# Where the first column piece of v comes from: the normalised rows, or x times scale

## The chip, the cores and the metric

The kernel runs on one core of a Trainium2 chip. The core has a matrix engine (TensorE, here PE, whose weight loads are listed as PEld), a vector engine (DVE), a scalar engine for activations (ACT), a small general engine (POOL) and queues that start DMA transfers between the chip's main memory and the core's own memory (the SP queue carries most of them). Each engine runs its own instructions in the order in which the program was written out, and waits where an operand isn't there yet. The metric is the device time of one execution in microseconds.

## The reference

Two token groups, 1024 prompt rows and 32 sample rows of 1024 channels, go through a two-layer encoder. Only the first mixer's first half matters here:

```python
mod = jax.nn.silu(c) @ w_ada[i] + b_ada[i]
sh1, sc1, gt1, sh2, sc2, gt2 = jnp.split(mod[:, None, :], N_MOD, axis=-1)
h = rmsnorm(x, g_norm[i, 0]) * (1 + sc1) + sh1
z = jax.nn.gelu(h @ w_in)
u, v = jnp.split(z, 2, axis=-1)
v = rmsnorm(v, g_v)
```

`rmsnorm(x, g)` is x times the reciprocal root r of each row's mean square, times g. So a row of `h @ w` is r times (x times s) @ w, plus (shift @ w), where s = g * (1 + sc1) is one number a channel and the last term is the same row for every token of a group. Behind that come the gating of u by v, a pooling mixer in the second layer, and two squared-ReLU channel MLPs.

## The kernel before

**Arithmetic.** Each product of two matrices is made as three products in a reduced fp32 format: every operand is split into a high and a low half (`hh` and `hl` of the rows, `wh` and `wl` of the weights), and hh·wh, hl·wh and hh·wl are summed in PSUM. High halves are made on ACT, low halves on DVE as the difference.

**Tiles.** The 1056 rows stand channel by channel ("turned") in `acc` as three tiles: 384 rows, 384 rows, and 256 rows with the 32 sample rows. A tile has three row blocks, so there are nine, b = 0 to 8, of which block 8 is the sample. v has 2048 columns, in four pieces p of 512. One pair (p, b) is 24 products of 128 x 512 (8 channel blocks k, three products each), and 16 for block 8. The weights of a piece come as four quarters (p, q), of two channel blocks each.

**The order.** The start, up to the last part of the norm of tile 2, is written out by hand inside `tc.manual_schedule()` (from L991 on). Everything behind it is placed by a planner: it keeps a running estimate of PE's and DVE's time (`tick`, and the helpers of L66 to L84 through which nearly all DVE work goes, so that it is recorded under line 79), and puts work for later stages (`weave`: high and low halves of weights, slices of w_ada) between the products where DVE is thought to have time. Loads are issued in the order of one list, `stream`, as buffers come free (`issue`, L395).

**The start before, step by step.** The blocks of x are loaded in front (`add_x`), then for each quarter q the slice 4 + q of w_ada (scale), its slice q (shift) and a quarter of the weights. The conditions are passed through silu and turned (`turn_conditions`, csilT). A block of x is squared and summed on ACT (`x_squares`), and turned on PE in two halves of four transposes (`x_turn`, xT, L580), which DVE and ACT copy to `acc`. `first_norm(t)` makes the reciprocal root of each row (`spread`), puts these on the diagonal of a matrix (L730) and multiplies it with ones (pb_h, L732), which spreads them over all partitions; `apply` then makes, channel block by channel block, mt = x * scale * root on DVE, hh = mt + shift on ACT (L875) and hl on DVE. A slice of w_ada is 16 small products (ada, L477), a transposition on DVE (adas, L489) and eight small products (adat, L459), behind which coef (scale) or shift is made. `early_mm` (L973) makes the products of piece 0 for blocks 0 to 4 quarter by quarter as the norm proceeds; block 5 follows in one go (`v_mm`, L929 to L931), and `early_end` closes them (`v_end`: gelu, square and sum, store of vd by the SP queue, L941 to L943). The result tile `vt` of `v_end` has three buffers, and so has the small PSUM pool (`ps_ms`) that takes xT, ada, adat and pb_h. Behind the part by hand, `v_order` goes through piece 1 for blocks 0 to 5, pieces 0 and 1 for blocks 6 to 8, and then pieces 2 and 3.

Later slices of w_ada (from the ninth on) are made on DVE in place of PE: 16 multiplications by csil (aa), a transposition and a sum.

Of the kernel before, what the change touches and what calls it, by code (L numbers as in the profile page):

```python
# [15 lines left out]
P = 128  # L16
# [18 lines left out]
def tile_stream_encoder_step(  # L35
# [26 lines left out]
    act = nc.scalar.activation  # L62
# [10 lines left out]
    def on_dve(op, fixed, rate):  # L73
        def run(out, *args, **kw):
            n = 1
            for k in out.shape[1:]:
                n *= k
            time["dve"] += fixed + n / rate
            return op(out, *args, **kw)  # L79

        return run
# [98 lines left out]
    def load_vectors(i, part):  # L180
        at = sum(k for _, k in rows[i][: part.start])
        for ap, k in rows[i][part]:
            nc.scalar.dma_start(vec_rows[i][at : at + k, :P], ap)
            at += k
# [6 lines left out]
    def turn_conditions():  # L191
        raw = vec_rows[2]
        nc.vector.memset(csil32, 0.0)
        act(out=raw[0:16, P : 2 * P], in_=raw[0:16, :P], func=AF.Silu)

        act(out=raw[0:16, 2 * P : 2 * P + 1], in_=epsT[0:16, :], func=AF.Sqrt)
        pt = ps_ms("csilT")
        nc.tensor.transpose(pt[:, 0:16], raw[0:16, P : 2 * P], ident[0:16, 0:16])
# [3 lines left out]
    def turn_vectors():  # L202
        for raw, v in zip(vec_rows, vecs):
            n = v.shape[1]
            pt = ps_ms("rowT")
            nc.tensor.transpose(pt[:, :n], raw[:n, :P], ident[:n, :n])
            nc.vector.tensor_copy(v, pt[:, :n])
# [131 lines left out]
    for b in range(3):  # L339
        add_x(b)  # L340
    for q in range(4):
        for j in (8 + 2 * q, 9 + 2 * q, 2 * q, 2 * q + 1):
            add_ada(0, j)
        add_w(*v_item(0, q))
        if q == 0:
            for b in range(3, 6):
                add_x(b)
# [30 lines left out]
    state = {"issued": 0, "next": 0, "raw": 0, "used": 0, "folds": 0}  # L378
    deferred = []

    def in_raw(k):
# [5 lines left out]
    x_rows = [  # L387
        room("h", t, f"x_rows{t}")
        .rearrange("p k n -> p (k n)")[:, : ncol[t] // P * D]
        .rearrange("p (b k n) -> p b k n", k=KB, n=P)  # L390
        for t in range(NT)
    ]
    junk = room("l", NT - 1, "xsq")

    def issue():  # L395
        while state["issued"] < len(stream):
            k = state["issued"]
            kind, key, ap, shape = stream[k]
            if in_raw(k):
                if state["raw"] == RAW_SLOTS:  # L400
                    return
                state["raw"] += 1
                r = t_raw(f"raw{k}")
            elif kind == "x":
                r = x_rows[key // 3][:, key % 3] if key < 8 else junk[:, :, P : 2 * P]
            else:
                r = work.tile([P, 1024], F32, tag="W", bufs=W_SLOTS, name=f"raw{k}")
            if kind == "x":
                nr = P if key < 8 else DEC
                i = (nc.scalar if key == 2 else nc.sync).dma_start(  # L410
                    r[:nr], ap.rearrange("t (k n) -> t k n", n=P)
                )
            else:
                i = nc.sync.dma_start(r.rearrange("p (a b) -> p a b", a=shape[0]), ap)
            raws[k] = r
            loads[key] = i.ins
            state["issued"] += 1

    def do_w(key, r):
# [4 lines left out]
        if key == ("v", 0, 0):  # L424
            late_lo.append(lambda: tt(out=wl, in0=r, in1=wh.bitcast(F32), op=ALU.subtract))
        else:
            tt(out=wl, in0=r, in1=wh.bitcast(F32), op=ALU.subtract)
# [135 lines left out]
    def x_squares(b, r):  # L563
# [8 lines left out]
    def x_turn(b, r):  # L572
# [3 lines left out]
        for half in range(2):  # L576
# [8 lines left out]
            if half == 0 or t == 0:  # L585
# [5 lines left out]
    x_turns = deque()  # L591

    def do_x(b, r):
        x_squares(b, r)
        if b < 3:
            x_turn(b, r)
        else:
            x_turns.append(lambda: x_turn(b, r))
# [10 lines left out]
    def stream_step():  # L609
# [18 lines left out]
        if in_raw(k):  # L628
# [85 lines left out]

    def spread(t, ss, tag, out, dg):
# [5 lines left out]
        ts(ms[:, :nb], ss[:, :nb], 1.0 / D, EPS, op0=ALU.mult, op1=ALU.add)  # L721
        act(out=r0[:, :nb], in_=ms[:, :nb], func=AF.Sqrt)
        nc.vector.reciprocal(out=r0[:, :nb], in_=r0[:, :nb])
        tt(out=q[:, :nb], in0=r0[:, :nb], in1=r0[:, :nb], op=ALU.mult)
        stt(out=q[:, :nb], in0=q[:, :nb], scalar=-0.5, in1=ms[:, :nb], op0=ALU.mult, op1=ALU.mult)
        stt(out=r0[:, :nb], in0=q[:, :nb], scalar=1.5, in1=r0[:, :nb], op0=ALU.add, op1=ALU.mult)
        yield False
        pb = ps_ms(f"pb_{tag}")
        for b, (c0, w) in enumerate(blk):
            act(out=dg[:w, c0 : c0 + w], in_=ident[:w, :w], func=AF.Copy, scale=r0[:w, b : b + 1])  # L730
        for b, (c0, w) in enumerate(blk):
            mm(pb[:, c0 : c0 + w], ones[:w, :], dg[:w, c0 : c0 + w], start=True, stop=True)  # L732
        out.append(pb)
# [119 lines left out]
    def apply(t, l, cf, sh, r, keep=False):  # L853
        hh[t] = room("h", t, f"hh{l}_{cf}_{t}", F32R)
        hl[t] = room("l", t, f"hl{l}_{cf}_{t}", F32R)
# [40 lines left out]

    def products(ps, n, terms):
# [8 lines left out]

    ssqv = small.tile([P, 9, 4], F32, name="ssqv")
# [51 lines left out]
    h0, h1, h2 = (first_norm(t) for t in range(NT))  # L959

    def early_mm(bs, q):

        wh, wl = witem[("v", 0, q)]
        for second in (False, True):
            for b in bs:
                t, c0 = b // 3, b % 3 * P
                tick(0.46 if second else 0.92)
                for k in range(2):
                    kb = 2 * q + k
                    a_h, a_l = hh[t][:, kb, c0 : c0 + P], hl[t][:, kb, c0 : c0 + P]  # L970
                    w = slice(k * 512, k * 512 + 512)
                    for a in (a_h,) if second else (a_h, a_l):
                        mm(  # L973
                            early_ps[b],
                            a,
                            (wl if second else wh)[:, w],
                            start=kb == 0 and a is a_h and not second,
                            stop=kb == KB - 1 and second,
                        )
# [5 lines left out]
    def conditions(q):  # L985

        stream_to("ada", (0, 4 + q, 1))
        stream_to("ada", (0, q, 1))
        pe_folds.pop(0)()

    with tc.manual_schedule():  # L991
        load_vectors(2, slice(0, 2))
        issue()
        load_vectors(2, slice(2, 4))
        load_vectors(0, slice(0, 1))
        load_vectors(1, slice(0, 1))
        turn_conditions()
        stream_to("x", 1)
        turn_vectors()
        stream_to("x", 2)  # L1000
        next(h0)
        conditions(0)
        statistics(h0)
        stream_to("w", ("v", 0, 0))
        pe_folds.pop(0)()
        for q in range(4):
            next(h0)
            if q == 0:
                late_lo.pop()()
            early_mm((0, 1, 2), q)  # L1010
            if q == 0:
                stream_to("x", 5)
                next(h1)
                x_turns.popleft()()
                x_turns.popleft()()
                next(h1)
                x_turns.popleft()()
                statistics(h1)
            next(h1)
            if q < 3:  # L1020
                conditions(q + 1)
                stream_to("w", ("v", 0, q + 1))
                early_mm((3,), q)
                pe_folds.pop(0)()
                early_mm((4,), q)
                if q == 2:
                    stream_to("x", 6)
            else:
                early_mm((3, 4), q)
        stream_to("x", 8)  # L1030
        while x_turns:
            x_turns.popleft()()
        next(h2)
        ps = ps_ms("pv0_5")
        v_mm(ps, 0, 5, range(KB))
        next(h2)
        early_end((0,))
        stream_to("w", ("v", 1, 1))
        early_end((1, 2))
        stream_to("w", ("v", 1, 2))  # L1040
        early_end((3,))
        stream_to("w", ("v", 1, 3))
        early_end((4,))
        statistics(h2)
        v_end(ps, 0, 5)
# [13 lines left out]
    rv = small.tile([P, 9], F32, name="rv")  # L1059
    rms = small.tile([P, 9, 2], F32, name="rms")  # L1060

# [11 lines left out]
    v_order = [(1, b) for b in range(6)] + [(p, b) for p in range(2) for b in range(6, 9)]  # L1073
    v_order += [(p, b) for p in range(2, 4) for b in range(9)]
    time["dve"] = time["pe"] + 8.0
    for p, b in v_order:
# [8 lines left out]
        weave()  # L1085

# [55 lines left out]
    def sgu_group(g):  # L1142
        wt = sgu.tile([P, P], F32, tag="wt", bufs=2, name=f"wt{g}")
        nc.sync.dma_start(wt, sgu_w_s[0, g])
        bb = sgu.tile([P, P], F32, tag="bs", bufs=2, name=f"bs{g}")
        nc.scalar.dma_start(bb, sgu_b_s[0, g].partition_broadcast(P))
# [527 lines left out]
```

## Time and profile before

| | before |
|---|---|
| time, median of 3 | 2171.42 us (2170.09 to 2173.31) |
| time of the profiled execution | 2173.74 us |
| its span | 2171.7 us |
| PE busy | 2145.5 us |
| mean granted PE clock | 0.996 |
| first product of piece 0 starts | 19.77 us |
| first product of piece 1 starts | 77.47 us |
| first product of piece 2 with a weight of piece 2 starts | 142.68 us |

The profile gives busy times by engine, windows with the granted clock of PE (1.00 is full speed), and the order of instructions on an engine with their start and duration; a bracket behind an instruction tells the idle time ahead of it and what ended it. Where a row groups several instructions ("x2"), its duration goes from the first one's start to the last one's end. PE's instructions overlap, so the distance between their starts tells their cost.

### The profile page before, as it was taken

Reading aid. Unit: us, or ns where it says so; the run is one execution under the profiler, and the core shown is the slowest. Engines: PE = TensorE matmul, PEld = TensorE weight load, DVE = VectorE, ACT = ScalarE, POOL = GpSimd, SP = SyncE. Lnnn points to the kernel's source line nnn. Section 1 sums busy time; section 2 is a strip of 40 time slices with the busy share of each in tenths; the row PEclk is TensorE's granted clock in tenths of the full one; section 3 lists DMA queues with packets and bytes.
Section 4 is the critical chain, followed back from the end, with each engine's and each line's share of the span. In section 5 each row is a group of like instructions: output and inputs, shape, how many; then the busy total and the mean of one; then the engine's idle time right before and its main releaser. Section 6 shows DMA issues by size and latency. Waiting matters only on the chain.

```text
span 2171.7 us, 33210 instructions
## 1 busy us (share of the span) xinstructions
PE 2145.5 (99%) x13214; PEld 2078.1 (96%) x13214; DVE 1431.8 (66%) x2499; ACT 971.3 (45%) x1643; POOL 13.3 (1%) x30
## 2 busy tenths in 40 slices
PE   7999999999999999999999999999999999999998
PEld 5778899999999999999999999999999999999997
DVE  5688647566879548496747879869675554523377
ACT  4633422234447552323445566666555542313354
POOL 0000000000000000000000000000000000000001
PEclk9999999999999999999999999999999999999999
DMA  8386534343437454243645466565455552302255
GB/s 300 119 269 193 173 93 139 90 148 109 147 96 233 132 155 143 87 140 110 196 129 161 141 189 182 171 191 158 141 161 158 157 155 68 98 20 78 69 139 125
DMA packets 383262, 312.95 MB, mean 144 GB/s; under 512 B 39458, under 2 KB 346346, under 8 KB 383108
## 3 DMA queue, kind: packets, MB, share of 16 engines
q1 hardware_dynamic: 380452, 308.64, 46.8%
q8 instruction: 103, 1.69, 0.3%
q10 hardware_dynamic: 2144, 1.41, 0.2%
q0 software_dynamic: 512, 0.79, 0.1%
q14 instruction: 51, 0.42, 0.1%
HBM read 278.95 MB, written 31.84 MB: 143 GB/s over the span
## 4 chain that ended last, share of the span: by engine, by line
PE 93%; DVE 3%; DMA 2%; ACT 1%; issue 1%; ACTq 0%; DVEq 0%; SPq 0%
PE pg L902 11%; PE pg L903 11%; PE pg L904 11%; PE pf L902 11%; PE pf L904 11%; PE pf L903 11%; PE po L902 3%; PE po L903 3%; PE po L904 3%; PE pu L902 3%; PE pu L904 3%; PE pu L903 3%; PE pv L929 2%; PE pv L930 2%; PE pv L931 2%; PE pp L1532 1%
## 5 line engine op out<-in xcount | busy, mean ns | idle before, releaser
L902 PE MATMUL pg<-fh,wh_dn 128*128 128x384 f32 (+1 forms) x1536 | 495.8, 323 | 0.0
L902 PE MATMUL pf<-hh,wh_up 128*128 128x384 f32 (+1 forms) x1536 | 494.4, 322 | 0.0
L903 PE MATMUL pf<-hl,wh_up 128*128 128x384 f32 (+1 forms) x1536 | 493.1, 321 | 0.0
L904 PE MATMUL pf<-hh,wl_up 128*128 128x384 f32 (+1 forms) x1536 | 492.9, 321 | 0.2 <-DVE wl_up L79 0.2
L903 PE MATMUL pg<-fl,wh_dn 128*128 128x384 f32 (+1 forms) x1536 | 492.6, 321 | 0.4 <-DVE fl L79 0.4
L904 PE MATMUL pg<-fh,wl_dn 128*128 128x384 f32 (+1 forms) x1536 | 492.5, 321 | 0.0
L79 DVE TENSOR_TENSOR wl_up<-raw,wh_up 128x1024 fp32r<-128x1024 f32 x152 | 185.9, 1224 | 165.4 <-ACT wh_up L422 165.4
L902 PEld LDWEIGHTS pg<-fh,wh_dn 128*128 128x128 f32 x1536 | 288.3, 188 | 1.5 <-ACT fh L1121 0.6
L903 PEld LDWEIGHTS pg<-fl,wh_dn 128*128 128x128 f32 x1536 | 288.3, 188 | 1.5 <-DVE fl L79 0.7
L904 PEld LDWEIGHTS pf<-hh,wl_up 128*128 128x128 f32 x1536 | 288.6, 188 | 0.5 <-DVE wl_up L79 0.5
L903 PEld LDWEIGHTS pf<-hl,wh_up 128*128 128x128 f32 x1536 | 288.3, 188 | 0.4
L902 PEld LDWEIGHTS pf<-hh,wh_up 128*128 128x128 f32 x1536 | 288.2, 188 | 0.4
L904 PEld LDWEIGHTS pg<-fh,wl_dn 128*128 128x128 f32 x1536 | 288.3, 188 | 0.0
L422 ACT ACTIVATE wh_up<-raw 128x1024 fp32r<-128x1024 f32 x152 | 161.2, 1060 | 279.9 <-PE pf L903 213.6
L79 DVE TENSOR_TENSOR acc<-acc,pg 128x384 f32<-128x384 f32 (+1 forms) x336 | 174.2, 519 | 146.3 <-PE pg L904 145.7
L422 ACT ACTIVATE wh_dn<-raw 128x1024 fp32r<-128x1024 f32 x152 | 160.8, 1059 | 202.9 <-PE pg L903 170.6
L79 DVE TENSOR_TENSOR wl_dn<-raw,wh_dn 128x1024 fp32r<-128x1024 f32 x152 | 186.0, 1224 | 82.4 <-ACT wh_dn L422 82.2
L79 DVE SCALAR_TENSOR_TENSOR aa<-raw,csil,aa 128x512 f32<-128x512 f32 (+1 forms) x364 | 203.5, 623 | 8.0 <-DMA raw<-in_w_ada_dram 7.9
L1295 ACT ACTIVATE r<-pf 128x384 f32<-128x384 f32 (+1 forms) x192 | 86.6, 451 | 201.9 <-PE pf L904 199.2
L79 DVE TENSOR_TENSOR fl<-r,fh 128x384 fp32r<-128x384 f32 (+1 forms) x192 | 100.3, 523 | 85.4 <-ACT fh L1121 84.3
L902 PE MATMUL pu<-hh,wh_u 128*128 128x384 f32 (+1 forms) x384 | 125.8, 328 | 0.0
L902 PE MATMUL po<-ush,wh_o 128*128 128x384 f32 (+1 forms) x384 | 123.5, 322 | 0.0
(263 smaller groups left out, 2927.2 us busy)
## 6 DMA issues: line engine op xcount, KB each, us to landing
raw<-in_ffn_w_up_dram SPq DMA_DIRECT2D x152, 512.0 KB, 3.9
raw<-in_ffn_w_down_dram SPq DMA_DIRECT2D x152, 512.0 KB, 3.5
raw<-in_w_ada_dram SPq DMA_DIRECT2D x96, 512.0 KB, 4.3
raw<-in_sgu_w_in_dram SPq DMA_DIRECT2D x40, 512.0 KB, 4.4
xd<-acc SPq DMA_DIRECT2D x8, 1536.0 KB, 7.8
raw<-in_sgu_w_out_dram SPq DMA_DIRECT2D x24, 512.0 KB, 4.0
xo_r<-xd SPq DMA_DIRECT2D x32, 384.0 KB, 3.4
vd<-vt SPq DMA_DIRECT2D x32, 256.0 KB, 4.5
```

The source lines that it names most:

```text
L79: return op(out, *args, **kw)
L422: act(out=wh, in_=r, func=AF.Copy)
L902: mm(ps[:, :n], wh, rh, start=i == 0, stop=False)
L903: mm(ps[:, :n], wh, rl, start=False, stop=False)
L904: mm(ps[:, :n], wl, rh, start=False, stop=i == last)
L929: mm(ps[:m, :], a_h, wh[:, o : o + 512], start=k == 0, stop=False)
L930: mm(ps[:m, :], a_h, wl[:, o : o + 512], start=False, stop=False)
L931: mm(ps[:m, :], a_l, wh[:, o : o + 512], start=False, stop=k == KB - 1)
L1295: act(out=r[:, :n], in_=ps[:, :n], func=AF.Relu)
L1532: mm(ps[:, :n], wg[:, k, e * P : (e + 1) * P], A(t, 2 * g + k), start=k == 0, stop=k == 1)
```

## The change

Piece 0 of blocks 0 to 5 is computed from x times scale, without root and shift. `scaled` makes the high half on ACT and the low half on DVE straight from the turned x. The roots enter when the sums are read: blocks 0 to 2 in `early_read` (ACT), 3 to 5 in `v_end` (DVE). The shift's share is one row: `shift_products` multiplies the split shift with the weights of piece 0 (16 products of two rows), `spread_shift` spreads it over all rows by a product with ones, and `v_end` adds it. For pieces 1 to 3, `full(t)` makes the complete norm of tiles 0 and 1 as before, later; tile 2 goes through `first_norm` as before.

Loads come as block 0 of x, scale slice 4, weights (0,0), then x 1 and 2, scale slice 5, weights (0,1), and so on; the four shift slices stand behind the last quarter. `x` goes through SP's queue only, vectors through a queue given as an argument. The buffer of a weight of piece 0 is held until its low half is made, which is at a place of its own (`late_lo`). The roots are made by one activation, Abs_reciprocal_sqrt, in place of Sqrt and a reciprocal. Dummy products (`warm`) stand on PE ahead of the first work and around the first scale slice.

By hand are now also placed: (1,0) to (1,3), the shift row between (1,0) and (1,1), the turns of blocks 6 to 8 behind (1,1) and (1,2), and the closing of blocks 0 to 5 among them. The planner's list begins with (1,4). `issue_after` keeps what the planner places on ACT and DVE during `v_order` behind the last ACT and DVE instruction of the part by hand. The two small loads of each gating group both go by SP's queue, behind the loads of weight (2,3).

```diff
+    def diagonals(t, r0, blk, dg, tag):
         pb = ps_ms(f"pb_{tag}")
         for b, (c0, w) in enumerate(blk):
             act(out=dg[:w, c0 : c0 + w], in_=ident[:w, :w], func=AF.Copy, scale=r0[:w, b : b + 1])
         for b, (c0, w) in enumerate(blk):
             mm(pb[:, c0 : c0 + w], ones[:w, :], dg[:w, c0 : c0 + w], start=True, stop=True)
-        out.append(pb)
+        return pb
+
+    def roots(r0, ms, q, ss):
+        ts(ms, ss, 1.0 / D, EPS, op0=ALU.mult, op1=ALU.add)
+        act(out=r0, in_=ms, func=AF.Abs_reciprocal_sqrt)
...
+    def scaled(t, ks, c0, w):
...
+        for k in ks:
+            act(
+                out=hh[t][:, k, c0 : c0 + w],
+                in_=A(t, k, c0, w),
+                func=AF.Copy,
+                scale=coef[:, 0, 0, 0, k : k + 1],
+            )
+        for k in ks:
+            stt(
+                out=hl[t][:, k, c0 : c0 + w],
+                in0=A(t, k, c0, w),
+                scalar=coef[:, 0, 0, 0, k : k + 1],
+                in1=hh[t][:, k, c0 : c0 + w].bitcast(F32),
+                op0=ALU.mult,
+                op1=ALU.subtract,
+            )
+
+    def full(t):
+        cp = t_c(f"r_h0_{t}")
+        pb = diagonals(t, rv[:, 3 * t : 3 * t + 3], [(c * P, P) for c in range(3)], cp, f"h0_{t}")
+        act(out=cp[:, : ncol[t]], in_=pb[:, : ncol[t]], func=AF.Copy)
+        yield False
+        yield from apply(t, 0, 0, 0, cp, keep=True)
...
     def v_end(ps, p, b):
         m = P if b < 8 else DEC
-        vt = t_x(f"vt{p}_{b}", [P, 512])
+        vt = early_vt.pop(b) if p == 0 and b in early_vt else t_x(f"vt{p}_{b}", [P, 512])
         z = ps
-        if b == 8:
+        if p == 0 and b < 3:
+            tt(out=vt, in0=vt, in1=bias[0], op=ALU.add)
+            z = vt
+            ps = bias[1]
+        elif p == 0 and b < 6:
+            stt(out=vt, in0=ps, scalar=rv[:, b : b + 1], in1=bias[0], op0=ALU.mult, op1=ALU.add)
+            z = vt
...
+    def spread_shift(got):
+        row, prow = got
+        pbias = ps_ms("pbias")
+        mm(pbias, ones[0:2, :], row[0:2, :], start=True, stop=True)
+        bias.append(work.tile([P, 512], F32, tag="aa", bufs=2, name="shift_rows"))
+        act(out=bias[0], in_=pbias, func=AF.Copy)
+        bias.append(prow)
...
+        warm(10)
         turn_conditions()
+        stream_to("x", 0)
+        x_turn(0)
+        turn_vector(0)
+        turn_vector(1)
+        slice_(4)
+        warm(3)
+        x_squares(0)
+        fold()
+        warm(3)
+        weights(0, 0)
+        scaled(0, (0, 1), 0, P)
+        early_mm((0,), (0, 1), False)
...
+        roots_of(0)
+        fold()
+        slice_(1)
+        early_ps.append(ps_ms("pv0_5"))
+        early_mm(rear, (0, 1), False)
+        f0 = full(0)
+        next(f0)
+        for b in front:
+            early_read(b)
+        fold()
+        early_mm(rear, (0, 1), True)
+        scaled(1, (2, 3), 0, 3 * P)
+        slice_(2)
+        early_mm(rear, (2, 3), False)
+        fold()
+        next(f0)
+        early_mm(rear, (2, 3), True)
+        scaled(1, (4, 5), 0, 3 * P)
+        slice_(3)
+        stream_to("x", 8)
+        weights(1, 0)
+        early_mm(rear, (4, 5), False)
+        fold()
+        next(f0)
+        early_mm(rear, (4, 5), True)
+        scaled(1, (6, 7), 0, 3 * P)
+        weights(1, 1)
+        early_mm(rear, (6, 7), False)
+        next(f0)
+        weights(1, 2)
+        early_mm(rear, (6, 7), True)
+        next(f0)
+        roots_of(1)
+        weights(1, 3)
+        f1 = full(1)
+        next(f1)
+        ps = [ps_dn(f"pv1_{b}") for b in range(3)]
+        v_mm(ps[0], 1, 0, range(KB))
+        next(f1)
+        next(f1)
+        row = shift_products()
+        spread_shift(row)
+        early_end((0,))
+        v_end(ps[0], 1, 0)
+        v_mm(ps[1], 1, 1, range(KB))
+        next(f1)
+        next(f1)
+        early_end((1,))
+        early_end((2,))
+        v_end(ps[1], 1, 1)
+        x_turn(6)
+        v_mm(ps[2], 1, 2, range(KB))
...
+    behind = ExitStack()
+    for e in ("act", "dve"):
+        behind.enter_context(tc.issue_after(last[e]))
+    v_order = [(1, b) for b in range(4, 6)] + [(p, b) for p in range(2) for b in range(6, 9)]
```

More of the change, by code (lines that the diff above doesn't have):

```diff
@@ L78, in run @@
             time["dve"] += fixed + n / rate
[L79 removed]
+            last["dve"] = op(out, *args, **kw).ins
         return run
@@ L200, in turn_conditions, with turn_vector @@
         nc.vector.tensor_copy(csil32[:, :, 0:NV], csil)
[L202 to L207, printed above, removed]
+    def turn_vector(i):
+        raw, v = vec_rows[i], vecs[i]
+        n = v.shape[1]
+        pt = ps_ms("rowT")
+        nc.tensor.transpose(pt[:, :n], raw[:n, :P], ident[:n, :n])
+        nc.vector.tensor_copy(v, pt[:, :n])
     gT = vecs[0]
@@ L627, in stream_step @@
         state["next"] += 1
-        if in_raw(k):
+        if k < first_ada and kind == "ada":
+            state["early"] -= 1
+        if in_raw(k) and not (kind == "w" and key[:2] == ("v", 0)):
             state["raw"] -= 1
@@ L720, in spread @@
         ms, r0, q = t_st(f"ms_{tag}"), t_st(f"r0_{tag}"), t_st(f"q_{tag}")
[L721 to L726, printed above, removed]
-        yield False
[L728 to L732, printed above, removed]
-        out.append(pb)
+        roots(r0[:, :nb], ms[:, :nb], q[:, :nb], ss[:, :nb])
+        yield False
+        out.append(diagonals(t, r0, blk, dg, tag))
         yield False
```

288 lines of the change are left out of this document (181 added, 107 removed).

## The prediction

> **What bounds the kernel now.** I read the page's first lines, then the windows of the start, then the order of each engine in time.
>
> ```profile
> span 2171.7 us, 33210 instructions
> PE 2145.5 (99%) x13214; PEld 2078.1 (96%) x13214; DVE 1431.8 (66%) x2499; ACT 971.3 (45%) x1643; POOL 13.3 (1%) x30
> ```
>
> TensorE (PE) is the bound: 2171.7 - 2145.5 = 26.2 us in which it does nothing. Only that, the time in which it works at a low clock, and work added to it can move the end. The windows (PE, weight load, DVE, ACT, POOL, granted clock, DMA share, GB/s) show where these lie:
>
> ```profile
> 20.00:30.00 10.00, 9.12 (x34) 6.88 (x34) 4.25 (x10) 5.21 (x12) 0.00 (x0) 0.69 1.08 385
> 34.00:36.00 2.00, 0.31 (x8) 0.00 (x0) 1.84 (x5) 1.82 (x3) 0.00 (x0) 1.00 1.08 386
> 36.00:38.00 2.00, 1.96 (x13) 1.59 (x14) 1.72 (x4) 0.00 (x0) 0.00 (x0) 0.59 1.09 385
> 38.00:40.00 2.00, 2.00 (x13) 1.21 (x12) 0.68 (x3) 0.00 (x0) 0.00 (x0) 0.56 1.09 382
> 88.00:120.00 32.00, 32.00 (x142) 26.37 (x141) 31.55 (x91) 14.65 (x39) 0.00 (x0) 1.00 0.54 166
> ```
>
> From 88 us on PE is full at full clock (32.00 of 32), so what there is to win lies ahead of it. DVE is full in that stretch too (31.55 of 32): if something there is put off, DVE is late first. Two rows show how the clock behaves: after 34 to 36, in which PE had 1.7 us without work, it ran at .59 and .56 for 4 us although PE was busy.
>
> So I compare the time at which each kernel reaches the third piece, (2,0): from there both have the same PE work. The marks of before, and the steps of PE:
>
> ```profile
> 19.77 0.79 PE L973 MATMUL pv<-wh_v,hh 128*128 128x512 f32 x1 [1.85 <-ACT hh L875]
> 55.57 1.93 PE L477 MATMUL ada<-raw,csil 128*32 128x256 f32 x32
> 57.32 0.22 PE L459 MATMUL adat<-adas,squares 128*32 128x4 f32 x8
> 68.20 2.04 PE L580 MATMUL xT<-ident,x_rows 128*128 128x128 f32 x16
> 72.27 0.39 PE L931 MATMUL pv<-wh_v,hl 128*128 128x512 f32 x1
> 76.38 0.39 PE L931 MATMUL pv<-wh_v,hl 128*128 128x512 f32 x1
> 76.60 0.94 PE L732 MATMUL pb_h<-r_h,ones 128*128 128x128 f32 x6
> 142.68 0.39 PE L930 MATMUL pv<-wl_v,hh 128*128 128x512 f32 x1
> ```
>
> From 72.27 to 76.38 lie 18 products: .2285 us each. A transpose is .127, a slice of w_ada .965, its second transposition .22, a diagonal .94. Until 142.68 before does 416 products (95.1), 70 transposes (8.8), 8 slices with their transpositions (9.5), three diagonals (2.8) and .6 of the rest: 116.8 us. 142.7 - 116.8 = 25.9 us are idle or half clock, and that is all that this change can touch.
>
> **The change part by part.** *Start.* One block of x, one scale slice and one column of scaled x are needed instead of three blocks, two slices and a whole norm.
>
> ```profile
> 1.06 0.32 DVE L129 CAST ones<-one 128x128 fp32r<-128x128 f32 x1
> 6.60 0.26 PE L198 MATMUL csilT<-ident,row 16*128 16x16 f32 x1 [6.60 <-ACT row L194]
> 6.79 3.68 PE L580 MATMUL xT<-ident,x_rows 128*128 128x128 f32 x16
> 13.40 3.45 PE L477 MATMUL ada<-raw,csil 128*32 128x256 f32 x32
> 37.12 0.63 PE L973 MATMUL pv<-wh_v,hh 128*128 128x512 f32 x1
> 37.55 0.63 PE L973 MATMUL pv<-wh_v,hl 128*128 128x512 f32 x1
> 56.71 0.45 DVE L489 STREAM_TRANSPOSE adas<-ada 128x256 f32<-128x256 f32 x1 [2.49 <-PE ada L477]
> 68.84 0.69 DVE L586 COPY acc<-xT 128x512 f32<-128x512 f32 x1 [4.58 <-PE xT L580]
> ```
>
> The ten warm products follow the cast (1.4) at half clock, .43 each: until 5.7. The turned conditions still come at 6.6 (their load); eight transposes at half clock are 1.8 (8.7), a copy .7 (9.4), 16 ada products between half clock (1.7) and full (1.0), 1.3 taken (10.7), the DVE transposition .45, the adat .22, coef .3 (two operations like 58.11 below) and the 128-column scaling some .35, with hops of .4: **12.4**, 7.4 earlier than 19.77. Bounds: 11.5 if the clock is full from the warm products on, 14 if they leave it cold. 2.7 us of needed work are done by then, so 9.7 us are lost.
>
> By the Trainium skill (TensorE: Matmul & The Clock Gate, Part 1) about 3.4 us of sustained work release the clock, which 4.3 us of warm products fulfil: the first product would come at 11.5 and the sum be .9 lower. No row before 6.6 shows the clock with PE at work, so the trace can't decide between the two.
>
> *Six blocks of piece 0, and seven quarter joints.* Work: 144 products 32.9, 40 transposes 5.1, 7 slices 6.8, 7 adat 1.5, a diagonal .94: 47.2. At each joint the next products wait for adat, coef, a weight's high half and scaled x on ACT:
>
> ```profile
> 53.47 1.04 ACT L422 ACTIVATE wh_v<-raw 128x1024 fp32r<-128x1024 f32 x1
> 58.11 0.16 DVE L79 SCALAR_TENSOR_TENSOR coef<-coef,vec 128x4 f32<-128x4 f32 x1
> 58.22 1.23 DVE L79 TENSOR_TENSOR wl_v<-raw,wh_v 128x1024 fp32r<-128x1024 f32 x1
> 59.46 1.14 DVE L79 SCALAR_TENSOR_TENSOR mt<-acc,coef,r_h 128x384 f32<-128x384 f32 x2
> 60.10 1.15 ACT L875 ACTIVATE hh<-mt,shift 128x384 fp32r<-128x384 f32 x2 [4.55 <-DVE mt L79]
> 60.75 1.15 DVE L79 SCALAR_TENSOR_TENSOR hl<-mt,shift,hh 128x384 fp32r<-128x384 f32 x2 [0.15 <-ACT hh L875]
> 72.13 0.91 ACT L730 ACTIVATE r_h<-ident,r_h 128x128 f32<-128x128 f32 x3 [0.84 <-DVE r_h L79]
> ```
>
> Between nothing (covered by the low products, 6 × .2285 = 1.37) and .3 + 1.04 + .57 = 1.9; I take 1.4, as most joints have no cover behind adat: 9.8. Blocks end at 12.4 + 47.2 + 9.8 = **69.4**.
>
> *First wait: the second diagonal.* It stands ahead of (1,0) on PE, and waits for the reciprocal roots of tile 1, which stand on DVE behind all four parts of tile 0's full norm. From the third shift slice's adat to these roots DVE has 4 × (1.14 + 1.15) = 9.2, two low parts of scaled x 2.3, a transposition .45, two shifts .3, three low halves of weights 3.7, roots .8: 16.8, and 19.6 with its waits for ACT; PE has 42 products 9.6, a slice and an adat: 10.7. ACT then needs .91 for the diagonals. 19.6 + .9 - 10.7 = 9.8, of which two quarter joints (2.8) are counted above, and .4 of hops: **7.4**. Bounds: 16.8 + .9 - 10.7 - 2.8 = 4.2 if DVE never waits for ACT, 10.8 if the joints don't overlap with it and the last high half (1.04) stands ahead of the diagonals on ACT. The clock then falls: 4 us at .575, as at 36 to 40, cost 1.7 (bound: 10 us at .69, as at 20 to 30, 3.1). With diagonal and (1,0): 69.4 + 7.4 + 1.7 + .94 + 5.5 = 84.9.
>
> *Shift row.* 16 products 3.7 and a ones-product in fp32 on 512 columns, by the diagonals' .94 on 384 some 1.2: 4.9 us of new PE work. With two hops (.4, .9) and (1,1), 5.5: 96.6; the first half of block 6's turn, .5: 97.1.
>
> *Second wait: block 6's turn.* Two of three small PSUM buffers are held (block 5's sums, the shift row), so its second half waits for the first half's copy, which stands last on a busy DVE list.
>
> ```profile
> 73.06 1.28 ACT L941 ACT_TABLE_LOAD   x1
> 81.54 0.60 ACT L942 ACTIVATE pv<-vt 128x512 f32<-128x512 f32 x1
> 82.75 0.52 SPq L943 DMA_DIRECT2D vd<-vt  x1
> 85.50 0.60 ACT L941 ACTIVATE vt<-pv 128x512 f32<-128x512 f32 x1 [2.29 <-DMA vd<-vt]
> ```
>
> From the ones-product: copy .6, add .6, table 1.28, gelu .6; then the gelu of (1,0) needs a buffer that the first store frees (82.75 to 85.50: 2.7), .6 and a square .8; only then ACT scales columns 4 and 5 (.6), and DVE does their low half, the last part (1.15 + .6 + 1.15), two adds 1.2, the copy .7, hops .5. Sum 13.1 after the ones-product's end at 91.1: 104.2, **7.1** of wait (4.4 if that store is back in time, nothing only if PE itself comes 7 us later; 8.5 with a hop of .1 more at each of fourteen steps). Then 1.7 cold, .5, (1,2), turns 2.7, (1,3), 13 products of (1,4) 3.0, .7 and the third diagonal: P = **124.8**.
>
> *Third wait: the weights of piece 2.* DVE's later parts are now kept behind the written-out part, so eight slice halves that before lay among the norm of tile 2 come in one row after it:
>
> ```profile
> 86.76 0.39 ACT L893 ACTIVATE r_h<-pb_h 128x288 f32<-128x288 f32 x1
> 88.30 0.71 ACT L875 ACTIVATE hh<-mt,shift 128x256 fp32r<-128x256 f32 x2
> 95.73 0.65 DVE L79 SCALAR_TENSOR_TENSOR hl<-mt,shift,hh 128x256 fp32r<-128x256 f32 x2
> 109.35 0.35 DVE L79 TENSOR_SCALAR aa<-raw,csil 128x256 f32<-128x256 f32 x1
> 116.60 0.35 DVE L79 TENSOR_SCALAR aa<-raw,csil 128x256 f32<-128x256 f32 x1
> 126.10 2.36 DVE L79 TENSOR_TENSOR wl_v<-raw,wh_v 128x1024 fp32r<-128x1024 f32 x2 [0.68 <-ACT wh_v L422]
> ```
>
> (aa rows are slices of w_ada on DVE, 16 operations each.) Before, that low half was ready at 128.5, 14 us ahead of 142.68. After: copy .4, table, gelu and square 2.7, norm 8 × 1.47 + .7 (a part is 1.30 if DVE alone counts, 2.01 if nothing overlaps), four rows of 7.25 (109.35 to 116.60) 29.0, low half 1.23, hops .5: P + 45.6 = **170.4**. PE has 163 products 37.2 and 2.0 of waits: idle 6.4, bounds 5 and 10, and 1.7 of cold clock. Lag 170.4 - 142.7 + 1.7 = **29.4**.
>
> *At nothing:* the loads. The 18 blocks of .52 MB up to the last weight of piece 0 take 24.5 us at the 385 GB/s of 20 to 30, some 28 with their start; three joints and three quarters after 12.4 that weight is wanted, at about 38. If the first transfers start 10 us late this cover is gone, and each further us is one on PE. x now stands on one queue, ahead of the weights that its turns precede anyway, so the order of use is the order of arrival. The reciprocal root replaces two operations on three columns by one; if its table has to be loaded anew it is another 1.28 (row 73.06) ahead of the diagonals, within the first wait's upper bound. The extra scaled halves (8 × .57 on DVE a tile) are in the joints and in the 16.8.
>
> **Sum.** Profiled execution 2173.7 (span 2171.7 and 2 around it), 2.3 above the median of 2171.4. 2173.7 + 29.4 - 2.3 = **2201**.
>
> **Rivals.**
> 1. *Only the first wait stays* (the turn and the weights hidden). For it: each hangs on one chain of a dozen steps, and the second is no wait if its norm parts run beside (1,1), the third if half of the slices' 29.0 are done beside the norm's waits for ACT. P = 124.8 - 8.8 = 116.0, (2,0) at 116.0 + 39.2 = 155.2, lag 12.5: **2184**. Against: DVE keeps its order, in which the slices stand behind the norm.
> 2. *The clock falls at the joints too.* For it: 1.7 us of idle sufficed at 34 to 36. Three falls of 1.7: **2206**. By the Trainium skill (same page, Part 1) it takes an idle window of 3.4 us, which no joint has; the row at 34 to 36 speaks against that figure.
> 3. *Faster: DVE keeps up.* If DVE's list ahead of the second diagonal is done when PE ends six blocks (its 16.8 us begun while PE has 16.8 left, not 10.7), and the other waits are covered, then 9.7 + 4.9 = 14.6 are lost, with some .4 a joint 17.4, against 25.9: -8.5, **2163** (2160 without joints). It decides from DVE's third shift slice: 6 us earlier. Against: that slice hangs on PE itself.
> 4. *No change:* the waits vanish, the joints stay: 14.6 + 9.8 + 1.5 = 25.9: **2171**.
> That the warm products leave the clock cold is inside the start's bounds (+1.6).
>
> **How the numbers follow.** Forecast .48, rival 1 .20, rival 2 .12, rival 3 .13, no change .07. The forecast's own range is 2194 to 2209 (first wait -3.2 to +3.4, third -1.4 to +3.6, three cold phases +1.4 each, start -.9 to +1.6, a part of each; a second wait of nothing is on rival 1's side). Leaving out rivals 3 and 4 (.20) sets the low end under rival 1 with its bounds, 2180; the high end 2209. Within 0.2% (4.3 us, what such a measurement can tell) falls rival 4 alone: faster .13, same .07, slower .80.
>
> **What would show it.** First product 11.5 to 14. PE idle ahead of the second pb_h at some 70 us, with DVE on mt and hl; idle between the two halves of block 6's turn; wl_v of (2,0) after 160 us, behind unbroken rows of aa. If (2,0) starts before 150, the second and third wait were mispriced; if before 142, rival 3.

## The result, and the profile after

The changed kernel takes 2204.19 us (median of 4, 2201.76 to 2204.32) against 2171.09 before (median of 4): a ratio of 1.0148, 95% interval 1.0131 to 1.0166. It is slower by 33 us, where 2201 was predicted (range 2180 to 2209).

The first lines of the page after:

```profile
span 2200.0 us, 33336 instructions
PE 2162.4 (98%) x13248; PEld 2082.2 (95%) x13248; DVE 1443.6 (66%) x2519; ACT 987.4 (45%) x1672; POOL 14.3 (1%) x32
```

The span grew by 28.3 us. PE's idle time went from 26.2 to 37.6 us (+11.4), and its busy time by 16.9: 6.1 of dummy products, 4.8 of the shift row, and 3.4 of work at a low clock (8.2 us lost to it from 12 us on, 4.8 before, by windows of 1 us); the other 2.6 no row shows. The profiled execution was the fastest of the four (2201.76), and the one of before lay above its median; so the profiles differ by 28, the medians by 33.

The order of PE in time, after (start, duration, engine, line, operation, count, and the idle time ahead with what ended it), at the places that the prediction named:

```profile
1.36 4.21 PE L1106 MATMUL pv<-ones 128*128 128x512 f32 x10 [1.36 <-DVE ones L132]
5.86 1.09 PE L605 MATMUL xT<-ident,x_rows 128*128 128x128 f32 x8
...
11.26 0.50 PE L1038 MATMUL pv<-wh_v,hx 128*128 128x512 f32 x1
...
27.98 0.50 PE L1038 MATMUL pv<-wh_v,hx 128*128 128x512 f32 x1 [1.19 <-ACT hx L65]
28.63 0.64 PE L1038 MATMUL pv<-wh_v,lx 128*128 128x512 f32 x1 [0.15 <-DVE lx L82]
29.07 0.63 PE L1038 MATMUL pv<-wh_v,hx 128*128 128x512 f32 x1
...
68.48 1.52 PE L1038 MATMUL pv<-wl_v,hx 128*128 128x512 f32 x6
75.65 1.65 PE L741 MATMUL pb_h<-r_h,ones 128*128 128x128 f32 x6 [5.65 <-ACT r_h L65]
76.95 0.77 PE L989 MATMUL pv<-wh_v,hx 128*128 128x512 f32 x1
...
83.93 0.40 PE L1073 MATMUL prow<-wh_v,parts_of_shift 128*2 128x512 f32 x1
...
88.47 1.12 PE L1087 MATMUL pbias<-shift_row,ones 2*128 2x512 f32 x2 [0.68 <-ACT shift_row L65]
...
95.11 0.60 PE L605 MATMUL xT<-ident,x_rows 128*128 128x128 f32 x4
101.89 1.12 PE L605 MATMUL xT<-ident,x_rows 128*128 128x128 f32 x4 [6.18 <-DVE acc L611]
...
163.10 0.40 PE L982 MATMUL pv<-wl_v,hs 128*64 128x512 f32 x1
166.14 0.73 PE L989 MATMUL pv<-wh_v,hx 128*128 128x512 f32 x2 [2.64 <-ACT wh_v L65]
167.41 0.50 PE L989 MATMUL pv<-wh_v,hx 128*128 128x512 f32 x1 [0.54 <-ACT pv L65]
168.79 0.80 PE L990 MATMUL pv<-wl_v,hx 128*128 128x512 f32 x1 [0.88 <-DVE wl_v L82]
```

The first product comes 8.5 us earlier than before (11.26 for 19.77), and at full clock. That lead is more than eaten by three waits in brackets, 5.65, 6.18 and 2.64 + 0.54 + 0.88, each with some microseconds of half clock behind it (products .43 us apart instead of .23). What PE waited for stood late in the order of DVE and ACT:

```profile
62.69 0.16 DVE L82 TENSOR_TENSOR shift<-adat,vec 128x4 f32<-128x4 f32 x1 [1.11 <-PE adat L482]
...
73.96 0.16 DVE L82 TENSOR_SCALAR rms<-ssx 128x3 f32<-128x3 f32 x1
...
94.63 0.60 ACT L65 ACTIVATE vt<-pv 128x512 f32<-128x512 f32 x1 [1.70 <-DMA vd<-vt]
...
96.52 1.15 DVE L82 SCALAR_TENSOR_TENSOR lx<-mt,shift,hx 128x384 fp32r<-128x384 f32 x2 [4.51 <-ACT hx L65]
...
101.15 0.68 DVE L611 COPY acc<-xT 128x512 f32<-128x512 f32 x1
...
138.18 0.61 DVE L82 TENSOR_SCALAR aa<-raw,csil 128x256 f32<-128x256 f32 x2
...
165.03 1.06 ACT L65 ACTIVATE wh_v<-raw 128x1024 fp32r<-128x1024 f32 x1 [0.91 <-DMA raw<-in_sgu_w_in_dram]
...
167.53 1.21 DVE L82 TENSOR_TENSOR wl_v<-raw,wh_v 128x1024 fp32r<-128x1024 f32 x1
```

DVE begins the roots of tile 1 only at 73.96, 4 us after PE has finished (70.0). Block 6's copy at 101.15 stands behind the norm, which stands behind ACT's gelu, which waited for a store; DVE itself stood idle for 4.51 us there. From 138.18 on DVE works without a break, nearly all of it on the slices (aa), and the third wait has one more link than was predicted: the weights of piece 2 themselves come late (DMA at 165.03), since the slices hold the three buffers into which they are loaded.

How much of it stays to the end is read from the start of the gating stage, of which a view by tile gives the first and the last start (246.7 before, 276.2 after: 29.5 us later, as is the rest of the kernel):

```profile
L1213 PE MATMUL psp<-wr,vl x256: 270/275/356, 246.7 to 629.5; 128*128 128x128 f32 x128
```

```profile
L1405 PE MATMUL psp<-wr,vl x256: 270/275/377, 276.2 to 659.1; 128*128 128x128 f32 x128
```

Behind this mark the kernels hardly differ: from it to the end the profiles of all eleven kernels here take 1923.8 to 1925.9 us (1925.0 before, 1923.8 after). So the experiments are read by it and by the end of (1,8), of which the start of the last product is given: 142.2 before and 163.1 after. Each is one profile of one execution, and single executions of one kernel differ by 2.6 us here (2201.76 to 2204.32) and by 4.8 in one of the runs below (2182.64 to 2187.47), so a difference of 2 us alone says little.

### The profile page after: what moved, and what is told of

It is laid out like the page before. It is cut to its first block, busy times and chain, and to the rows that moved or that the text cites. A ratio compares the mean times of both kernels' runs of the same rounds, so it can differ in the third digit from the quotient of the medians.

```text
span 2200.0 us, 33336 instructions
## 1 busy us (share of the span) xinstructions
PE 2162.4 (98%) x13248; PEld 2082.2 (95%) x13248; DVE 1443.6 (66%) x2519; ACT 987.4 (45%) x1672; POOL 14.3 (1%) x32
## 4 chain that ended last, share of the span: by engine, by line
PE 90%; DVE 5%; DMA 3%; ACT 2%; issue 1%; ACTq 0%; DVEq 0%; SPq 0%
PE pg L958 11%; PE pf L958 11%; PE pg L960 11%; PE pg L959 11%; PE pf L960 11%; PE pf L959 11%; PE pu L958 3%; PE pu L960 3%; PE pu L959 3%; PE po L959 3%; PE po L958 3%; PE po L960 3%; DVE aa L82 2%; PE psp L1405 1%; PE pp L1724 1%; PE pv L1038 1%
## 5 line engine op out<-in xcount | busy, mean ns | idle before, releaser
L960 PE MATMUL po<-ush,wl_o 128*128 128x384 f32 (+1 forms) x384 | 123.1, 321 | 0.0
```

Of the source, the lines that this page charges most:

```text
L960: mm(ps[:, :n], wl, rh, start=False, stop=i == last)
```

## The experiments

All start from the changed kernel; where an edit stands on top of another, the text says so.

**Roots of tile 1 early.**

```diff
         roots_of(0)
+        roots_of(1)
...
         early_mm(rear, (2, 3), True)
+        f1 = full(1)
+        next(f1)
...
-        roots_of(1)
         weights(1, 3)
-        f1 = full(1)
-        next(f1)
```

> The reciprocal roots of tile 1 are made with those of tile 0, and the second diagonal stands on PE behind rear quarter 1 instead of ahead of (1,0). If the first wait is DVE's list ahead of the roots: the 5.65 us of idle ahead of the second pb_h and its cold 1.5 us go, and (1,0) starts at about 70 us instead of 76.95. It won't all stay: the shift row needs the split shift, which stands on DVE and ACT behind the third and fourth low half and two norm parts of tile 1 (by rows of the changed kernel until some 80.4), so the row starts at about 80.5 instead of 83.93 and the end is 3 to 4 us earlier, span 2196 to 2197. If instead (1,0) itself is bound by the weights or the rows of tile 0 (the rival), it has idle time of its own between its products and the shift row moves by less than 1 us.

```profile
75.25 0.50 PE L989 MATMUL pv<-wh_v,hx 128*128 128x512 f32 x1 [0.32 <-ACT wh_v L65]
76.51 0.50 PE L990 MATMUL pv<-wl_v,hx 128*128 128x512 f32 x1 [0.76 <-DVE wl_v L82]
81.40 0.58 PE L1073 MATMUL prow<-wh_v,parts_of_shift 128*2 128x512 f32 x1 [3.45 <-DVE parts_of_shift L82]
87.97 1.12 PE L1087 MATMUL pbias<-shift_row,ones 2*128 2x512 f32 x2 [0.68 <-ACT shift_row L65]
```

The first wait is gone, and (1,0) starts right behind the six blocks; yet 4.5 us of waits stand in its place, the largest at the shift row, where it was expected. What the expectation missed is the price of that wait: the clock fell again, from the row's start to the ones-product's wait 5.9 us pass (87.97 - .68 - 81.40) and not 3.9, and (1,8) ended only .7 us earlier, at 162.4. Even that is chance: the clock stayed up at 28 us in this execution, which is worth 1.5 us. The gating stage starts at 278.2, later by 2.0. The wait had been put off, not taken away: what counts here is the order of DVE's list, not the place of the diagonal.

**Roots early, and the split of the shift where it is ready.** As in the run before, and `parts_of_shift` is made right behind the last shift slice:

```diff
         early_mm(rear, (4, 5), False)
         fold()
+        split = shift_parts()
...
-        row = shift_products()
+        row = shift_products(split)
```

> As with the roots early, and the split of the shift into its two halves is made where the last shift slice is ready, so the shift row waits for nothing on DVE. If DVE's list only moved the first wait to the shift row in the run before: (1,0) starts at 70 and ends at 77 to 78, the row follows at once, the ones-product starts at some 82 instead of 88.5, and (1,8) ends 5.5 to 7 us earlier than 163.1, with the third wait unchanged: span 2193 to 2197. Rival: ACT and DVE between 82 and 120 us set the time whatever PE does before; then block 6's turn waits 3 us or more longer than 6.2 and (1,8) ends less than 3 us earlier.

```profile
82.51 1.12 PE L1091 MATMUL pbias<-shift_row,ones 2*128 2x512 f32 x2 [0.68 <-ACT shift_row L65]
...
95.93 1.12 PE L605 MATMUL xT<-ident,x_rows 128*128 128x128 f32 x4 [6.20 <-DVE acc L611]
```

```profile
L1410 PE MATMUL psp<-wr,vl x256: 270/275/377, 270.3 to 653.1; 128*128 128x128 f32 x128
```

The ones-product starts at 82.51 (88.47), (1,8) ends at 155.9 (7.2 earlier), and the gating stage starts at 270.3, 5.9 earlier; its span is 2195.0. Block 6's turn waits for the same 6.20 us as before, only earlier. So the first wait is worth about 6 us, once nothing else hangs on the end of that list. (The clock stayed up at 28 us here, but fell behind the joint at 66 us, so the two nearly cancel.)

**Block 6's turn early.**

```diff
+        x_turn(6)
         row = shift_products()
...
         v_end(ps[1], 1, 1)
-        x_turn(6)
```

> Block 6 is turned between (1,0) and the shift row instead of behind (1,1); nothing else is moved. If the second wait is the first half's copy standing last on DVE's list behind the norm of tile 1: its 6.18 us and the cold 1.5 to 2 us behind it go, (1,2) follows (1,1) directly at about 96, and the span falls by 5 to 8 us to 2192 to 2195 (up to 3 us may come back as a wait of block 7's turn for a PSUM buffer). If it is the PSUM pool alone that is short (the rival), the shift row's own products then wait by 4 us or more for a buffer, and the span falls by less than 3.

```profile
104.36 0.66 PE L605 MATMUL xT<-ident,x_rows 128*128 128x128 f32 x4 [0.79 <-DVE acc L611]
105.80 0.43 PE L605 MATMUL xT<-ident,xsq 32*128 32x32 f32 x4 [0.79 <-ACT prow L65]
106.62 0.43 PE L605 MATMUL xT<-ident,xsq 32*128 32x32 f32 x4 [0.38 <-DVE acc L611]
110.91 0.33 PE L209 MATMUL rowT<-ident,row 40*128 40x40 f32 x1 [3.87 <-ACT acc L65]
```

Neither came true: the 6.18 us are gone from block 6's turn, and 5.83 us (.79 + .79 + .38 + 3.87) stand at the turns behind it; the shift row waits 1.08 us, not 4. (1,8) ends 2.3 us earlier, and the gating stage starts at 276.2 as after the change. The copy was only the last link; what PE waits for is ACT, which closes blocks 0 to 2 and, from 106.89 to 110.3, sums the squares of blocks 6 to 8 ahead of the copy that PE needs, wherever the turns stand. DVE, the releaser in the bracket, is not full here: it stands idle for 4.52 us up to 98.94, for ACT.

**Norm of tile 1 ahead of the closing.** The last two parts of `f1` go up to the first two, and the split of the shift is early:

```diff
         next(f1)
         next(f1)
+        next(f1)
+        next(f1)
         row = shift_products(split)
...
         v_mm(ps[1], 1, 1, range(KB))
-        next(f1)
-        next(f1)
```

> The last two norm parts of tile 1 are put ahead of the closing of block 0 on ACT and DVE (and the split of the shift early, so that the shift row isn't behind them). If the second wait is DVE's list held up by ACT (gelu of (1,0) behind the first store, then the rows of those parts): the wait between the halves of block 6's turn falls from 6.2 to under 1.5 us, its cold clock goes, and (1,8) ends 5 to 8 us earlier, span 2192 to 2196. Rival, as when the turn alone was moved: the chain of closing the blocks on ACT is long in itself, and the wait comes back at the turns of blocks 7 and 8 or at the third diagonal; then (1,8) ends less than 3 us earlier.

```profile
95.24 0.66 PE L605 MATMUL xT<-ident,x_rows 128*128 128x128 f32 x4 [0.79 <-DVE acc L611]
...
102.60 0.43 PE L605 MATMUL xT<-ident,xsq 32*128 32x32 f32 x4 [0.35 <-DVE acc L611]
```

```profile
L1410 PE MATMUL psp<-wr,vl x256: 270/275/377, 270.2 to 653.0; 128*128 128x128 f32 x128
```

The wait falls to .79, the clock stays up, (1,8) ends at 153.7 (9.4 earlier, some 1.5 of them from a joint that kept its clock), and the gating stage starts at 270.2, 6.0 earlier. So the second wait was DVE's norm held up behind ACT's gelu and its store, as the prediction's chain had it; the experiment before shows that taking its last step out is not enough. Of the gain 3.4 us came back behind (1,8): some 1.7 as a longer stretch of low clock (.92 and .91 from 140 to 180 us, 1.00 and .91 after the change), the rest as a wait of 2.06 us instead of .42 at the gating stage.

**Weights of piece 2 ahead of the slices.**

```diff
-    some_ada(8)
     for p in range(2, 4):
         w_vpiece(p)
-        some_ada(8)
+        some_ada(12)
```

> In the list of loads the weights of piece 2 stand ahead of the four slices of w_ada that stood between pieces 1 and 2; 12 slice halves then follow piece 2 and 12 piece 3. If the third wait is DVE doing those slices first: the waits at 163 to 169 us (2.64 + 0.54 + 0.88) and the one of 0.8 behind them go with some 1 us of cold clock, the first product of piece 2 with its low half starts at about 163.5, and the span is 5.5 to 6.5 us shorter, 2193.5 to 2194.5. If the weights were late for another reason (DMA), the waits stay and the span is within 1 us of 2200.

```profile
164.10 0.39 PE L981 MATMUL pv<-wl_v,hs 128*64 128x512 f32 x1
164.33 0.40 PE L988 MATMUL pv<-wh_v,hx 128*128 128x512 f32 x1
```

Piece 2 follows (1,8) without a gap. The gating stage starts at 271.0 (5.2 earlier), the span is 2195.2, .7 above what was expected: (1,8) ended 1.0 later in this execution, and a wait of 1.0 us for a low half of the u weights is new. That the slices, which have to be done somewhere, are the cause of it was not looked at.

**The planner's work not kept behind.**

```diff
     for e in ("act", "dve"):
-        behind.enter_context(tc.issue_after(last[e]))
+        pass
```

> The planner's ACT and DVE work is no longer kept behind the part written by hand; the slices of w_ada then lie among the norms of tiles 1 and 2 on DVE. The third wait goes as in the run with piece 2 first (5.5 to 6.5 us). The thirteen multiplications placed ahead of a low half of tile 1's norm take 5.2 us and a transposition 0.7 where DVE had 4.5 us of idle time, so block 6's turn comes 1 to 3 us later. Span 2195 to 2198. Rival: keeping the work behind costs nothing, and letting it in only delays the norms: span above 2201.

```profile
L1405 PE MATMUL psp<-wr,vl x256: 270/275/356, 267.4 to 649.8; 128*128 128x128 f32 x128
```

The gating stage starts at 267.4, 8.8 us earlier, and the span is 2191.6: more than expected. The wait at block 6's turn grew to 8.10 as it was thought to, but (1,8) ended no later (162.9): the clock stayed up at 28 us in this execution (1.5 us), and the 2.2 us of waits between 134 and 139 us are gone. From the end of (1,8) to the gating stage 104.5 us pass before, 113.1 after, 106.9 with the weights ahead, and 104.5 here: behind (1,8), keeping the planner's work behind cost the whole 8.6.

**No dummy products.** The three calls of `warm` are left out.

> The sixteen dummy products ahead of the first work are left out. If they bring the clock up, as the changed kernel's first product at 11.26 us (at full clock) suggests: without them the transposes, the first slice and the first products run at half clock, 1.8 for 1.1, 1.7 for 1.1, and some 4 us of products at half clock behind the start; the six blocks end 1.5 to 3.5 us later, against up to 2 us of PE time of the dummies that are gone from between the first slice and the first product. Net (1,0) starts 0 to 3 us later, span 2200 to 2205. Rival: the clock comes up by the transposes alone, nothing changes but the 2 us of dummies, and (1,0) starts up to 1 us earlier.

```profile
5.65 1.97 PE L605 MATMUL xT<-ident,x_rows 128*128 128x128 f32 x8
...
12.19 0.80 PE L1038 MATMUL pv<-wh_v,hx 128*128 128x512 f32 x1 [0.92 <-ACT hx L65]
...
29.67 0.50 PE L1038 MATMUL pv<-wh_v,hx 128*128 128x512 f32 x1 [1.19 <-ACT hx L65]
...
75.89 1.65 PE L741 MATMUL pb_h<-r_h,ones 128*128 128x128 f32 x6 [5.64 <-ACT r_h L65]
```

The first eight transposes take 1.97 us instead of 1.09, the first product comes at 12.19 and takes .80 as before the change; by 28 us the kernel is 1.7 behind (29.67 for 27.98). So the dummies are worth 1.7 us up to there. They are hidden at the second diagonal (75.89 for 75.65), because this execution kept its clock at the joint behind 28 us and the other did not. Another 2.6 us are lost behind (1,8); whether that has to do with the dummies was not tried, but the run with the roots early, which has them, loses 2.7 there too.

**All three taken away:** roots, split and norm early, and nothing kept behind.

> The roots and the split early, the norm parts of tile 1 ahead of the closing of block 0, and the planner's work not kept behind. If the three waits are separate and what the theory says of them holds: first -6, second -5 to -8, third -8.6, so the first block of the gating stage starts at 276.2 - 20 = 254 to 258 us and the median is 2180 to 2186. That is still above the kernel before (2171): what is left are the extra 4.9 us of the shift row and 10 to 11 us of joints, against 8.5 gained at the start. If the waits hang together (slices of w_ada fill the DVE time that the norms need), the sum is less and the median is above 2188.

Median 2183.49 (2182.64 to 2187.47), ratio to before 1.0051 (1.0034 to 1.0068). The gating stage starts at 255.9, 20.3 earlier than after the change; the parts alone gave 5.9 + 6.0 + 8.8 = 20.7. The three are separate, and add up within what single executions can tell: in all four of these profiles the clock stayed up at 28 us, a gain of 1.5 us that none of the edits was made for.

```profile
L1410 PE MATMUL psp<-wr,vl x256: 269/275/357, 255.9 to 638.2; 128*128 128x128 f32 x128
```

```profile
86.05 1.29 PE L1091 MATMUL pbias<-shift_row,ones 2*128 2x512 f32 x2 [4.28 <-ACT shift_row L65]
```

What is left to the kernel before, 9.2 us, has its largest single wait here: the shift row's copy stands on ACT behind the norm parts that were moved up.

**And that wait too.** On top of the last: the two norm parts between the shift row and the closing, one slice's second transposition inside its quarter's low products, and one scaling ahead of a norm part.

```diff
-        early_mm(front, (2, 3), True)
+        early_mm((0,), (2, 3), True)
         fold()
+        early_mm((1, 2), (2, 3), True)
...
+        scaled(1, (6, 7), 0, 3 * P)
         next(f0)
         early_mm(rear, (4, 5), True)
-        scaled(1, (6, 7), 0, 3 * P)
...
-        next(f1)
-        next(f1)
         row = shift_products(split)
         spread_shift(row)
+        next(f1)
+        next(f1)
```

> On top of all three waits taken away: the last two norm parts of tile 1 go between the shift row and the closing of block 0 (in the run before, the row's copy stood behind them on ACT, and the ones-product waited 4.28 us), the second transposition of scale slice 6 stands inside the low products of its quarter instead of behind them, and the last scaled columns of tile 1 are made ahead of a norm part. By the theory (order on DVE and ACT alone keeps PE waiting): the ones-product's wait falls below 1 us, the joint at 28 us (1.19) and the one at 66 us (1.35) each by 0.5 to 1.2, up to 2 us come back at block 6's turn; the gating stage starts 4 to 7 us earlier than 255.9, and the median is 2176 to 2180. It would beat the kernel before only if no joint were left, which this does not reach. Rival: DVE is full from 63 to 86 us, so that what PE does not wait for at the ones-product it waits for at the next norm part; then the median is above 2181.

```profile
75.12 0.79 PE L989 MATMUL pv<-wh_v,hx 128*128 128x512 f32 x1 [1.23 <-ACT wh_v L65]
...
84.74 1.12 PE L1091 MATMUL pbias<-shift_row,ones 2*128 2x512 f32 x2 [0.68 <-ACT shift_row L65]
...
101.47 0.66 PE L605 MATMUL xT<-ident,x_rows 128*128 128x128 f32 x4 [1.55 <-DVE acc L611]
...
105.70 0.33 PE L209 MATMUL rowT<-ident,row 40*128 40x40 f32 x1 [2.19 <-ACT acc L65]
```

DVE's list in that stretch goes on like this:

```profile
73.63 1.15 DVE L82 SCALAR_TENSOR_TENSOR lx<-mt,shift,hx 128x384 fp32r<-128x384 f32 x2 [0.16 <-ACT hx L65]
75.10 1.23 DVE L82 TENSOR_TENSOR wl_v<-raw,wh_v 128x1024 fp32r<-128x1024 f32 x1 [0.32 <-ACT wh_v L65]
```

The median is 2185.64 (ratio 1.0059, 1.0045 to 1.0073), no better than the last, as the rival had it. The waits that were aimed at are gone (.68 at the ones-product; the joints at 28 and 66 us; (1,0) starts at 68.1), and others stand in their place: 2.6 us inside (1,0), with half clock behind them until the shift row (.51 from 78 to 82 us), 5.5 at the turns, and a clock of .66 from 100 to 110 us. They stand at the weights of (1,0) and at the turns, and not, as the rival said, at the next norm part. DVE is busy for 16.9 of the 19 us from 63 to 82, and its idle time there is that of hops to ACT and back (.15 to .34); so PE, arriving earlier, finds the same work undone. No version tried beats the kernel before.

## Why the prediction was right, step by step

- **Start:** 12.4 foreseen (bounds 11.5 to 14), 11.26 measured, just below the bounds. The clock was full from the transposes at 5.86 on (eight in 1.09 us, not 1.8; 1.97 without the dummies). The value that the prediction gave by the Trainium skill (TensorE: Matmul & The Clock Gate, Part 1), 11.5, was the better one. The turned conditions came at 5.73 and not at 6.6, which lets the start lie below even that.
- **Six blocks:** end foreseen at 69.4, measured 70.0. The joints were mis-sized, 11.5 us instead of 9.8: 70.0 - 11.26 - 47.2. Of these 4.0 are idle (53.97 of 58 us busy between 12 and 70), some 1.5 low clock; the rest lies where the operation or its operands change, with no bracket or a short one: from a quarter's first high product to its second some .65 us pass instead of .23, and from the start of six low products to the next operation 1.6 instead of 1.37. What causes it was not tried.
- **First wait:** 7.4 and 1.7 of clock foreseen, 5.65 and 1.9 measured (76.95 to 83.93 is 7.0 for 5.5, and the diagonal .4); DVE's list as described. The first two experiments show that it is the order of that list, and not the diagonal's place.
- **Shift row:** 4.9 foreseen; 83.93 to 87.6 and 88.47 to 89.5 are 4.8.
- **Second wait:** 7.1 foreseen, 6.18 measured. The chain was right, its last link too narrow a name for it: with block 6 turned early the wait stayed, with the norm parts early it went.
- **Third wait:** its terms as listed add up to P + 46.3, not P + 45.6, so the forecast should have read 171.1, and 2201.5 instead of 2200.8 at the end. (2,0)'s first low product came at 168.79. The idle time foreseen there was 6.4 (bounds 5 and 10); 4.06 were measured, and 1.2 at two later places. With the clock 8.1 were foreseen, and 8.6 measured up to the gating stage: these 5.3 of waits, 1.5 of low clock (.94 and .89 between 160 and 180), and 1.8 that no row shows. The link over the loads was missed: the prediction prices no load of piece 2, and its weights came late (165.03).
- **Sum:** lag 29.4 foreseen, 29.5 at the gating stage, 28.3 in the span. That these agree so closely is partly luck, as errors cancel: the end of (1,0) came 1.0 us earlier than foreseen, the third diagonal 2.4 earlier (122.4 for 124.8), but the end of (1,8) only .7 earlier (163.3 for 164.0), since the 163 products between took some .237 us each and not .2285. The median of 2204.19 is 3 above 2201. The change in the medians is 33.1 us and in the profiles 28.3: the profiled execution was the fastest of its kernel, and no step held what the other three lose.
- **The rivals:** that only the first wait stays, that DVE keeps up, and that nothing changes all fell with the traces. That the clock falls at the joints came true at one joint in this execution (28.6 to 32), for about 1.5 us: from 27.98 to the diagonal at 49.08 pass 21.1 us, and 19.65 in the run with the planner's work let in (28.13 to 47.78), which kept its clock.

## What to carry to other kernels

A start that needs less input moves the first product forward, but the end only if the engines that prepare the later work get it done as much earlier. Here the scaled halves were made in addition to the full ones, some 9 us more for DVE, and the full norms came late in its order: in the changed kernel DVE is busy for 18.5 of the 44 us from 12 to 56, and for 21.6 of the 27 from 56 to 83. Whether work of the second stretch could be done in the first was not tried.

When a wait is to be removed, look at what stands ahead of the named releaser on its own engine, and at what that waits for in turn. Moving the instruction that waits (the diagonal, block 6's turn) only moved the wait. Moving what the releaser stood behind (the split of the shift together with the roots, the norm parts) took away about 6 us each time, with the same work on DVE and ACT. Where the engine is nearly full, as DVE is from 63 to 82 us in the last run, a further change of order gained nothing. And a rule that keeps background work behind the critical part takes away the idle time of DVE in which that work was nearly free (block 6's wait grew from 6.2 to 8.1 us): it cost 8.6 us, the largest single item.

## What the runs showed of the hardware

A wait of 1.19 us at 28 us, the same in the profiles of the changed kernel and of eight of its variants, was followed by half clock in three of the nine and not in the others: 28.6 to 32.3 us in the profile shown (products .43 apart), none in the six with the roots early, the norm early, without dummies, or with the planner's work let in (.23 apart). A longer wait need not do it: the kernel before waited for 1.59 us at 86.67 and went on at full clock.

```profile
86.67 0.50 PE L930 MATMUL pv<-wl_v,hh 128*128 128x512 f32 x1 [1.59 <-DVE wl_v L79]
87.00 0.39 PE L931 MATMUL pv<-wh_v,hl 128*128 128x512 f32 x1
```

The Trainium skill (TensorE: Matmul & The Clock Gate, Part 1) speaks of an idle window of about 3.4 us that runs freely; a free-running window would explain that it depends on the execution, but here 1.2 us of idle time were enough. The 1.5 us that it makes at 28 us may be one source of the 2.6 us between executions of the same kernel; this was not tried.
